# A decoder layer on one core: three transposes moved from TensorE to VectorE and DMAs, the last FFN block in 512 columns, norm2's factor in ScalarE's copies

## The chip, the cores and the metric

The kernel runs on one core of one Trainium2 chip. The core has five engines that run their own instruction streams and meet at semaphores: TensorE (matmuls; PE in the profile, and PEld for its weight loads), VectorE (DVE), ScalarE (ACT), GpSimd (POOL) and SyncE (SP), whose queue issues nearly all DMAs here. The metric is the device time of one execution in microseconds. Lower is better.

## The reference

One layer on `x` of 256 tokens by 1024 channels, in float32:

- `h = rmsnorm(x)`, and `u = h @ W_in`, whose columns are the recurrent input and gate, q, k, v and two branch gates.
- Branch A: a causal depthwise convolution of width 4, a gated linear recurrence over positions, times the GELU of its gate.
- Branch B: attention with 8 heads of 128 channels. With 256 tokens and blocks of 256, it is plain causal softmax attention on normalised q and k.
- `merged = sigmoid(gA) * (A @ P_A) + sigmoid(gB) * (B @ P_B)` and `x = x + merged @ W_out`.
- `h = rmsnorm(x)`, `up = conv3(h @ W_up)` (causal, depthwise, width 3), `act = gelu(up) * (h @ W_gate)`, `x = x + act @ W_down`, with 2816 hidden channels.

## The kernel before, in words

**Matmuls in three parts.** Every float32 operand is split in a high part `hi` (rounded to the matmul type fp32r) and a rest `lo`; a product is three matmuls, high by high, high by low and low by high (`mm3`). Weights stream from HBM in chunks of 128 x 2048 (1 MB): `raw` is loaded, ScalarE copies it to `hi` and VectorE subtracts to get `lo` (`split_part`). There are three `raw`, four `hi` and three `lo` buffers. Activations are split the same way (`split2`).

**Token-major work and turning.** Most projections hold 128 tokens' activations as the stationary operand and pass 512 columns of weights (`tm_mm`; one chunk is 24 matmuls). Their result has tokens in the partitions, while the next product needs channels there, so it is turned. There are two ways. TensorE transposes 128 x 128 blocks against the identity, into a PSUM bank, from which it is split: this is done for the probabilities (`att_t`, three blocks a head, tile `pt`), for the gated sum (`m_t`, four groups of four blocks, tile `mT`) and for norm2's input (`norm2_t`, four groups of four, tile `h2T`). Or `turn` (L437) does it: VectorE transposes 32 x 32 blocks inside the partitions, four DMAs write the strips to DRAM with the partition groups exchanged, and one DMA reads all back. This is done for the recurrent input and gate, q, k, and for the FFN's up and gate products.

**Attention.** For each head, `att_s` makes scores and softmax, `att_t` (L790) the turned and split probabilities, and `att_o` (L800) the output, six matmuls into tile `o`. A head has 384 columns of probabilities, because the causal mask leaves out one block of four.

**norm2's factor.** The rows of `h` aren't scaled before the FFN. Their factor `rs2` is applied afterwards. For up, which has a convolution and a GELU, it is needed along the free axis of the turned product, so `norm2_bcast` (L993) builds a diagonal and multiplies by ones on TensorE (tile `rbfp`), and `pair_up` (L1022) multiplies the turned product by it. For the gate it is left until `add_out` (L1062), where the down product is scaled and added to `x`.

**FFN.** The 11 blocks of 256 hidden channels run in five pairs, each two chunks of up and two of gate in 512 columns (`pair_half`, L1071), and down projections two pairs later (`downs`, L1084). The eleventh block runs alone in `last_block` (L1093), near the end, with the weights as the stationary operand and 256 tokens as columns: 96 matmuls of 256 columns, tiles `upl` and `gtl`, whose results need no turning.

**The order.** All operations are recorded first and then issued by a list written out in the file, `ORDER` (L161): plain numbers are operations of the other engines, `+n` stands for the next n matmuls. TensorE's own order comes from `UNITS` (L34), and `AFTER` (L36) names the items that are recorded after a quarter of a unit (`"pr1.0": "O5"`). Each engine runs its part of the list strictly in order, SP too, so a DMA that waits holds those behind it.

Of the kernel before, what the change touches and what calls it, by code (L numbers as in the profile page):

```python
# [14 lines left out]
P = 128  # L15
S = 256
# [16 lines left out]
KEPT = {"upd": 2, "gtd": 2, "u": 1, "c": 2, "ah": 3, "al": 3}  # L33
UNITS = ("rx0 rx1 rx2 rx3 rg0 rg1 rg2 rg3 k0 k1 k2 k3 ri0 q0 q1 ri1 ga0 ga1 q2 q3 v0 v1 ga2 ga3 v2 v3 gb0 "  # L34
         "gb1 gb2 gb3 pr0 pr1 pr2 pr3 pa0 pa1 pa2 pa3")
# [37 lines left out]
    "ga2.2": "s22 S0 P3",  # L73
# [3 lines left out]
    "ga3.2": "lc1 P1 lb0",  # L77
    "ga3.3": "s26",
    "v2.1": "P0 qrs1 S4",
    "v2.2": "O3 s27 s28",  # L80
    "v2.3": "ld1",
    "v3.2": "S5",
    "gb0.0": "P2",
    "gb0.1": "s29",
    "gb1.0": "gelu0 P4",
    "gb1.3": "s30 S6",
    "gb2.1": "S7",
    "gb2.2": "O2 lc0",
    "gb2.3": "O1 s31 s32 ld0",
    "gb3.0": "ya0",  # L90
    "gb3.1": "P5 ys0",
    "gb3.2": "O4",
    "pr0.0": "P7 sb0 s33",
    "pr0.2": "sa1 ya1",
    "pr0.3": "ys1",
    "pr1.0": "O5",
    "pr1.1": "s34",
    "pr1.2": "sa0",
    "pr1.3": "s35",
    "pr2.0": "P6",  # L100
    "pr2.1": "s36",
    "pr2.2": "O6",
    "pr2.3": "O0",
    "pr3.0": "s37",
    "pr3.3": "sb1",
    "pa1.0": "O7",
    "pa2.1": "m0",
    "pa3.2": "s38",
    "wo.0": "s39 m1",
    "wo.4": "m2",  # L110
    "wo.5": "s40",
    "wo.6": "m3",
    "wo.12": "n00",
    "wo.13": "n10",
    "wo.14": "s41",
    "up00.0": "s42 n01",
    "up00.2": "n11",
    "gt00.0": "s43",
    "gt00.3": "s44",
    "up01.3": "s45 s46",  # L120
    "gt01.2": "s47",
    "gt01.3": "bcast2",
    "up10.0": "ur0 s48",
    "up10.1": "s49",
    "up11.0": "s50",
    "up11.2": "fu0",
    "gt10.0": "s51",
    "gt10.1": "s52 gr0",
# [24 lines left out]
    "dn5.2": "gr4",  # L153
    "dn5.3": "s71",
    "dn7.0": "fg4",
    "last.2": "s72",
# [5 lines left out]
0-2 +1 3-4 +1 5 +1 6 +1 8 +1 7 +1 9 +1 11 +2 10 25 +1 12 30 +1 26-27 +1 14 +1 28 33 +1 29 +1 13 31 +2 32 +2 34 +1  # L162
35 +3 15 +7 36 +2 41 +3 19 +3 37 63 +1 42 +1 39 +3 43 +1 40 +1 17 38 +3 44 +1 49 +2 18 +3 45 64 50 +1 47 +4 51 46
+2 16 48 +3 52 +1 57 +4 53 +1 58 +1 55 +4 59 54 +2 56 +3 60 +7 66 +4 68 +1 67 +5 69 +3 99 +3 65 +5 70 100 +5 71 +5
72 +1 98 73 +1 74 +1 75 +1 76 +1 77 +1 78 104 +1 79-80 +1 81 +1 82 +1 83 +4 84 +1 105 +2 85 +4 116 +4 86 +1 103 +3
# [6 lines left out]
+6 188 228 +1 235 +4 189 +1 308 +2 242 190 +3 191 +2 162 240 +1 192 243 +2 244 247 +1 248 193 239 +1 249-250 +1  # L172
245 251 +2 246 +1 252 271 +2 272 +1 253 +1 229 +2 254 232 +1 309 +2 233 255 +2 230 +1 256 +2 322 +1 257 +2 231 +1
258 307 +2 234 +1 259 +3 260 273 +1 274-275 +1 276 108 261 +3 262 297 +2 323 +1 109 +1 263 329 +2 110 +3 277 +1
111 +3 112 +1 278 +6 299 279 +1 301 +1 321 +3 280 +2 332 330 +2 281 +3 282 +3 283 312 +2 311 302 +1 284 328 314 +2
264 313 305 285 +2 316 303 265 +1 286 315 +1 304 +1 317 +1 266 306 287 +1 318 +1 118 +1 288 +2 333 267 347 +1 289
+1 268 +2 194 269 +3 195 +2 298 196 +3 197 +1 300 +1 270 +1 198 +1 354 331 +1 355-356 +1 357 291 358 +3 290 359
# [8 lines left out]
+3 472 +1 391 +1 428 392 +1 393 +1 476 +3 478 +7 466 +1 473-474 467 +1 439 +2 468 +3 469 +1 527 470 +2 471 +5 484  # L186
+3 485 +2 479 +1 492 +3 494 +2 499 +6 486 528 +1 477 +3 496 +2 429 497 +2 537 +2 487 +1 539 +4 500 +3 507 +9 540
+1 502 498 +1 488 +1 503 +2 210 +1 489 +1 490-491 +2 431 +6 493 432 +4 495 +4 509 +2 510 +3 532 508 +12 504 538 +1
# [8 lines left out]
639 +3 655 +1 657 +9 668 653 +1 669-670 +1 671 +1 672 +1 673 +1 674 +1 675 +1 676 +1 658 +1 660 +9 677 +1 656 678  # L197
# [102 lines left out]
def trunk_layer(ctx: ExitStack, tc: tile.TileContext, xT, x, vec, win_fm, win_tm, wri, wpr, wpa,  # L300
# [58 lines left out]
    c_wo = [add(wout[c]) for c in range(4)]  # L359

    NP = NF // 2
    c_up, c_gt, c_dn = {}, {}, []
    for p in range(NP):
        for c, kh in ((c_up, 0), (c_gt, 0), (c_up, 1), (c_gt, 1)) if p == 0 else (
                (c_up, 0), (c_up, 1), (c_gt, 0), (c_gt, 1)):
# [835 lines left out]
```

## Time and profile before

| | us |
|---|---|
| median of 3 runs (435.06 to 435.16) | 435.13 |
| the profiled execution | 435.01 |
| its span in the trace | 433.2 |
| TensorE busy | 428.4 |
| VectorE busy | 326.8 |
| ScalarE busy | 256.9 |
| GpSimd busy | 50.1 |

The rows below name a line, an engine, an operation and tiles (`out<-in`). Nearly every operation is issued from one line of a helper, L296, so tiles tell the operations apart. Matmuls overlap in TensorE's pipeline: the duration of one is longer than the distance to the next. In the chain of waits a row has the start, the time until the next piece of the chain, the engine, the tile and the number of instructions merged.

### The profile page before, as it was taken

How to read it: one execution, taken by the hardware profiler on the slowest of the kernel's cores; microseconds unless marked ns; L12 is line 12 of the kernel's file. 1: busy time of each engine (PE TensorE's matmuls, PEld its weight loads, DVE VectorE, ACT ScalarE, POOL GpSimd, SP SyncE). 2: the span in 40 equal slices, each digit the busy share in tenths (PEclk: the TensorE clock that was granted, in tenths of full speed). 3: DMA queues.
4: the chain of work that ended last, by engine and by line, in shares of the span. 5: the costliest groups of instructions: out<-in, count | busy, mean ns of one | idle time of the engine just before them, and what ended most of it. 6: DMA issues, size and time to landing. Idle time of an engine off the chain costs nothing.

```text
span 433.2 us, 5466 instructions
## 1 busy us (share of the span) xinstructions
PE 428.4 (99%) x2044; PEld 360.0 (83%) x2044; DVE 326.8 (75%) x426; ACT 256.9 (59%) x285; POOL 50.1 (12%) x101
## 2 busy tenths in 40 slices
PE   8999999999999999999999999999999999999996
PEld 8888888888888888888888888888888888888985
DVE  3877499799888898985666896496979766767643
ACT  4687596886779999963431453357455555355410
POOL 0021007767660000000000000000000000000000
PEclk9999999999999999999999999999999999999999
DMA  7998944889991752274454466888789787697202
GB/s 259 404 385 243 360 153 147 269 292 326 372 358 52 276 194 97 98 290 130 163 194 141 151 220 202 288 288 300 238 264 328 256 285 245 211 317 249 97 2 97
DMA packets 32826, 100.06 MB, mean 231 GB/s; under 512 B 3104, under 2 KB 13472, under 8 KB 29088
## 3 DMA queue, kind: packets, MB, share of 16 engines
q1 hardware_dynamic: 32656, 99.71, 67.1%
q8 instruction: 16, 0.26, 0.2%
q14 instruction: 10, 0.08, 0.1%
q10 hardware_dynamic: 144, 0.00, 0.0%
HBM read 89.22 MB, written 10.49 MB: 230 GB/s over the span
## 4 chain that ended last, share of the span: by engine, by line
PE 97%; DMA 1%; DVE 0%; SPq 0%; ACT 0%; issue 0%
PE acc L296 14%; PE up L296 13%; PE gt L296 13%; PE pr L296 5%; PE gb L296 5%; PE yo L296 5%; PE ga L296 5%; PE v L296 5%; PE pa L296 5%; PE q L296 5%; PE k L296 5%; PE rg L296 5%; PE rx L296 4%; DMA raws<-in_win_fm 1%; PE gtl L296 1%; PE upl L296 1%
## 5 line engine op out<-in xcount | busy, mean ns | idle before, releaser
L296 DVE TENSOR_TENSOR lo<-raw,hi 128x2048 fp32r<-128x2048 f32 (+1 forms) x72 | 160.0, 2224 | 27.2 <-issue 9.5
L296 ACT CAST hi<-raw 128x2048 fp32r<-128x2048 f32 (+1 forms) x69 | 128.4, 1863 | 87.0 <-PE up L296 11.5
L296 PE MATMUL up<-hi,h2h 128*128 128x512 f32 x80 | 31.4, 393 | 0.0
L296 PE MATMUL up<-hi,h2l 128*128 128x512 f32 x80 | 31.1, 389 | 0.0
L296 PE MATMUL acc<-hi,fah 128*128 128x512 f32 x80 | 31.1, 389 | 0.0
L296 PE MATMUL acc<-lo,fah 128*128 128x512 f32 x80 | 31.1, 389 | 0.0
L296 PE MATMUL gt<-hi,h2l 128*128 128x512 f32 x80 | 31.1, 389 | 0.0
L296 PE MATMUL gt<-hi,h2h 128*128 128x512 f32 x80 | 31.1, 389 | 0.0
L296 PE MATMUL gt<-lo,h2h 128*128 128x512 f32 x80 | 31.1, 389 | 0.0
L296 PE MATMUL acc<-hi,fal 128*128 128x512 f32 x80 | 31.1, 389 | 0.0
L296 PE MATMUL up<-lo,h2h 128*128 128x512 f32 x80 | 31.1, 389 | 0.0
L296 ACT ACT_TABLE_LOAD x14 | 18.0, 1283 | 3.1 <-PEq L1191 1.2
L296 DVE SCALAR_TENSOR_TENSOR fc<-fu,pv,fc 128x255 f32<-128x255 f32 (+1 forms) x40 | 17.0, 475 | 2.0 <-ACT fc L296 1.9
L296 POOL TENSOR_TENSOR rsq<-rsq 128x8 f32<-128x8 f32 x32 | 17.1, 533 | 11.8 <-DVE rsq L296 9.6
L296 PEld LDWEIGHTS acc<-hi,fal 128*128 128x128 f32 x80 | 15.0, 188 | 3.2
L296 PEld LDWEIGHTS gt<-hi,h2h 128*128 128x128 f32 x80 | 15.0, 188 | 3.1
L296 PEld LDWEIGHTS up<-hi,h2l 128*128 128x128 f32 x80 | 15.0, 188 | 3.1
L296 PEld LDWEIGHTS acc<-hi,fah 128*128 128x128 f32 x80 | 15.0, 188 | 3.1
L296 PEld LDWEIGHTS gt<-lo,h2h 128*128 128x128 f32 x80 | 15.0, 188 | 3.1
L296 PEld LDWEIGHTS gt<-hi,h2l 128*128 128x128 f32 x80 | 15.0, 188 | 3.1
L296 PEld LDWEIGHTS up<-hi,h2h 128*128 128x128 f32 x80 | 15.0, 188 | 3.0
L296 PEld LDWEIGHTS acc<-lo,fah 128*128 128x128 f32 x80 | 15.0, 188 | 3.0
(228 smaller groups left out, 1041.3 us busy)
## 6 DMA issues: line engine op xcount, KB each, us to landing
raw<-in_win_fm SPq DMA_DIRECT2D x12, 1024.0 KB, 7.6
raw<-in_win_tm SPq DMA_DIRECT2D x12, 1024.0 KB, 6.2
raw<-in_wup SPq DMA_DIRECT2D x11, 1024.0 KB, 5.5
raw<-in_wgate SPq DMA_DIRECT2D x11, 1024.0 KB, 7.7
raw<-in_wdown SPq DMA_DIRECT2D x11, 1024.0 KB, 7.0
raw<-in_wpr SPq DMA_DIRECT2D x4, 1024.0 KB, 4.9
raw<-in_wpa SPq DMA_DIRECT2D x4, 1024.0 KB, 4.9
raw<-in_wout SPq DMA_DIRECT2D x4, 1024.0 KB, 4.8
```

The source lines that it names most:

```text
L296: getattr(engine, name)(*map(real, a), **{n: real(v) for n, v in k.items()})
```

## The change

The probabilities, half of the gated sum and half of norm2's input are no longer transposed by TensorE.

- `att_t` transposes 32 x 32 blocks on VectorE (384 columns) and writes four strips to DRAM; a new item `R` reads them back and a new item `Q` splits them. `att_o` reads the split probabilities, and writes its bank, in pieces of 32 or 64 columns, because the turned data stand in another order.
- The first half of the gated sum (`mt`, `mr`, `ms`) goes through `turn`. For that, the attention projections `pa0` and `pa1`, which complete the first half, run before `pr3`, and `m_t` remains for the second half.
- `W_out` is projected as a unit like the others (`wo0` to `wo3`), one half of its columns after the other, with its chunks loaded by columns in two DMAs. The first column half of `x` is still transposed by TensorE (`norm2_t`); the second goes through a turn (`ht`, `hr`) and is scaled by norm2's gain in four ScalarE copies (`hs`). The FFN's first units are put in an order that uses the second half last.
- `scaled` takes any factor; `ffn_half` uses it to copy up and gate products from PSUM times `rs2` on ScalarE before the turn, which then takes one transpose of 1024 columns in place of two of 512. `norm2_bcast`, with its two products on TensorE, is gone, `pair_up` copies in place of multiplying, and `add_out` adds without a factor.
- The last block's up and gate are one unit of 512 columns (256 of each) that follows the fifth pair and goes through a turn of its own (`lr5`, `fu`, `fg`).
- `UNITS`, `AFTER` and `ORDER` are new throughout.

```diff
-         "gb1 gb2 gb3 pr0 pr1 pr2 pr3 pa0 pa1 pa2 pa3")
+         "gb1 gb2 gb3 pr0 pr1 pr2 pa0 pa1 pr3 pa2 pa3 wo0 wo1 wo2 wo3")
...
+    def by_columns(w, c):
+        cs = slice(c // 2 * 512, c // 2 * 512 + 512)
+        return [w[2 * (c % 2) + j].rearrange("p (k c) -> p k c", k=2)[:, :, cs] for j in range(2)]
...
+            return [(n[:2], int(n[2]), int(n[3])) for n in "up00 gt00 up10 up01 gt01 up11 gt10 gt11".split()]
...
-    def scaled(name, ps):
-        r = half(name)
+    def scaled(r, ps, rs):
         for t in range(2):
-            nc.scalar.activation(r[:, t * 512:(t + 1) * 512], ps[t], AF.Copy, scale=rs1[:, t:t + 1])
+            nc.scalar.activation(r[:, t * 512:(t + 1) * 512], ps[t], AF.Copy, scale=rs[:, t:t + 1])
...
     def att_t(h):
         sm = heads[h]
-        ps = bank(f"pt{h}")
-        for b in range(3):
-            nc.tensor.transpose(ps[:, b * P:(b + 1) * P], sm[:, b * P:(b + 1) * P], ident)
+        d = small(f"pd{h}", 384)
+        nc.vector.transpose(d.rearrange("p (j u b) -> p u j b", j=4, u=3), sm.rearrange("p (u j b) -> p u j b", u=3, j=4))
+        mid = dram.tile([P, 384], F32, tag="pt", name=f"pm{h}")
+        m = mid.rearrange("(j a) (i f) -> i a j f", j=4, i=4)
+        for i in range(4):
+            nc.sync.dma_start(m[i], d[32 * i:32 * i + 32, :].rearrange("p (j f) -> p j f", j=4))
+        heads[h] = d, mid
+    def att_r(h):
+        nc.sync.dma_start(*heads[h])
+    def att_p(h):
         pth, ptl = small(f"pth{h}", 384, F32R), small(f"ptl{h}", 384, F32R)
-        split2(pth, ptl, ps[:, :3 * P])
+        split2(pth, ptl, heads[h][0])
...
+    def m_turn():
+        turn("mm", turned_m, sgb.half(0), "mr")
+    def m_split():
+        v = lambda a: a.half(0).rearrange("p (u i b) -> p u i b", u=8, i=4)
+        split2(v(mh), v(ml), by_tile(turned_m))
...
+    def h2_turn():
+        turn("hm", turned_h, [xs[:, t, halves[1]] for t in range(2)], "hr")
+    def h2_split():
+        m = half("h2p")
+        for k in range(4):
...
+            nc.scalar.activation(kt(m)[:, k, :].rearrange("p (t i b) -> p t i b", t=2, i=4), d, AF.Copy,
+                                 scale=pv[:, V_G2 + 4 + k:V_G2 + 5 + k])
+        split2(h2h.half(1), h2l.half(1), m)
...
-    def norm2_bcast():
+    def norm2_stats():
         nc.vector.tensor_add(ss2[:, 0, :], ss2[:, 0, :], ss2[:, 1, :])
         rsqrt(ss2[:, 0, :], rs2, 1.0 / D, 2)
-        for t in range(2):
-            nc.vector.tensor_scalar(dg[:, t, :], ident, rs2[:, t:t + 1], None, op0=OP.mult)
...
-            nc.tensor.matmul(ps[:, t * P:(t + 1) * P], ones, dg[:, t, :], start=True, stop=True)
-        nc.scalar.copy(rbf, ps[:, :S])
...
-            nc.vector.tensor_mul(plain(u, t), d[:, t], rb[:, t, None].to_broadcast([P, 4, 4, 32]))
+            nc.vector.tensor_copy(plain(u, t), d[:, t])
...
-        nc.vector.scalar_tensor_tensor(xs[:, t, cs], ps, rs2[:, t:t + 1], xs[:, t, cs], op0=OP.mult, op1=OP.add)
+        nc.vector.tensor_add(xs[:, t, cs], ps, xs[:, t, cs])
...
-                turn(f"{kind}m{p}", d, open_ps[kind, p], f"{kind[0]}r{p}")
+                turn(f"{kind}m{p}", d, scaled(keep("s", p), open_ps[kind, p], rs2), f"{kind[0]}r{p}")
...
-    def last_block():
-        pu, pg = fm_ps("upl"), fm_ps("gtl")
-        for ps, i in ((pu, c_up[NP]), (pg, c_gt[NP])):
...
+        if p == NP - 1:
+            for kh in range(2):
+                run(f"last{kh}", ffn_half("last", NP, kh, c_last[kh]))
```

More of the change, by code (lines that the diff above doesn't have):

```diff
@@ L72 @@
     "ga2.1": "rq1 S1 Tq1",
[L73 removed]
+    "ga2.2": "s22 S0",
     "ga2.3": "s23",
@@ L76 @@
     "ga3.1": "lb1",
-    "ga3.2": "lc1 P1 lb0",
+    "ga3.2": "lc1 lb0",
     "ga3.3": "s26",
[L79 to L83, printed above, removed]
+    "v2.1": "qrs1 S4",
+    "v2.2": "s27 s28 P3",
+    "v2.3": "ld1 R3",
+    "v3.2": "S5 R0 P1",
+    "gb0.0": "Q1 P2",
     "gb0.1": "s29",
-    "gb1.0": "gelu0 P4",
+    "gb1.0": "gelu0 R4",
     "gb1.3": "s30 S6",
     "gb2.1": "S7",
[L88 to L93, printed above, removed]
+    "gb2.2": "lc0 R5 P6",
+    "gb2.3": "s31 s32 ld0",
+    "gb3.0": "ya0 O2 Q5 R6",
+    "gb3.1": "ys0 Q6 P7",
+    "gb3.2": "R7",
+    "pr0.0": "sb0 s33",
     "pr0.2": "sa1 ya1",
-    "pr0.3": "ys1",
-    "pr1.0": "O5",
-    "pr1.1": "s34",
+    "pr0.3": "ys1 O5",
+    "pr1.1": "s34 O6",
     "pr1.2": "sa0",
     "pr1.3": "s35",
[L100 to L107, printed above, removed]
-    "pa3.2": "s38",
[L109 to L128, printed above, removed]
+    "pr2.1": "s36 O7",
+    "pa1.0": "s37",
+    "pa1.3": "mt sb1",
+    "pr3.2": "mr",
+    "pa2.3": "ms",
+    "pa3.2": "s38",
+    "v3.0": "Q3",
+    "v3.1": "P0",
+    "v3.3": "Q0 R1",
+    "gb0.2": "R2 O3",
+    "gb0.3": "Q2 P4",
+    "gb1.1": "O0",
+    "gb1.2": "Q4",
+    "gb2.0": "O1 P5",
+    "gb3.3": "O4 Q7",
+    "wo0.0": "s39",
+    "wo0.1": "m2",
+    "wo0.2": "m3",
+    "wo1.0": "s40",
+    "wo2.0": "n00 s41",
+    "wo2.1": "n10",
+    "up00.0": "s42 ht",
+    "up00.3": "s43 hr",
+    "gt00.2": "hs",
+    "up10.0": "s44 s45",
+    "up01.0": "s46 stats2",
+    "gt01.0": "s47",
+    "up11.0": "s48 ur0",
+    "gt10.0": "s49 s50",
+    "gt10.2": "s51 fu0",
+    "gt11.0": "s52 gr0",
     "gt11.1": "ur1",
@@ L152 @@
     "dn4.1": "s70 fg3",
-    "dn5.2": "gr4",
+    "dn5.2": "lr5 gr4",
     "dn5.3": "s71",
-    "dn7.0": "fg4",
-    "last.2": "s72",
+    "dn7.0": "fu fg fg4",
     "dn8.0": "s73",
@@ L381, in load_next @@
         raw[i] = wp.tile([P, 2048], F32, tag="raw", name=f"raw{i}")
+        if isinstance(stream[i], list):
+            n = 2048 // len(stream[i])
+            for a, src in enumerate(stream[i]):
+                d = raw[i][:, a * n:(a + 1) * n]
+                nc.sync.dma_start(d.rearrange("p (k c) -> p k c", k=2) if len(src.shape) == 3 else d, src)
+            return
         if len(stream[i].shape) == 3:
@@ L405, in advance @@
             j = split_tiles()
-            n, m = min(2048, stream[j].shape[-1] * (2 if len(stream[j].shape) == 3 else 1)), {4: 2}.get(j, 1)
+            src = stream[j]
+            n = 2048 if isinstance(src, list) else min(2048, src.shape[-1] * (2 if len(src.shape) == 3 else 1))
+            m = {4: 2}.get(j, 1)
             for a in range(m):
@@ L624, in rx_evac @@
         turned_x[g] = half(f"xd{g}")
-        turn(f"xm{g}", turned_x[g], scaled(f"xs{g}", rx_ps[g]), f"rx{g}")
+        turn(f"xm{g}", turned_x[g], scaled(half(f"xs{g}"), rx_ps[g], rs1), f"rx{g}")
     def rx_order(g):
@@ L816, in rg_evac @@
     def rg_evac(g):
-        turn(f"gm{g}", gr.half(g), scaled(f"gs{g}", rg_ps[g]), f"rgr{g}")
+        turn(f"gm{g}", gr.half(g), scaled(half(f"gs{g}"), rg_ps[g], rs1), f"rgr{g}")
     def gelu(h):
@@ L897, in run_unit @@
             for k4 in range(4):
-                tm_mm(ps, i, 4 * kh + k4, k4, *{"pr": (yah, yal), "pa": (ybh, ybl)}.get(kind, (xgh, xgl)),
-                      kind not in "qkv")
+                tm_mm(ps, i, 4 * kh + k4, k4, *{"pr": (yah, yal), "pa": (ybh, ybl), "wo": (mh, ml)}.get(kind, (xgh, xgl)),
+                      kind not in ("q", "k", "v", "wo"), *((m_stat,) if kind == "wo" else ()))
                 if kh and k4 == 3:
@@ L915, in trunk_layer @@
     for h in range(H):
-        for n, fn in (("S", att_s), ("P", att_t), ("O", att_o)):
+        for n, fn in (("S", att_s), ("P", att_t), ("R", att_r), ("Q", att_p), ("O", att_o)):
             item[f"{n}{h}"] = lambda fn=fn, h=h: fn(h)
-    for n in range(4):
+    for n in (2, 3):
         item[f"m{n}"] = lambda n=n: m_t(n)
+    item["mt"], item["ms"] = m_turn, m_split
     def run(name, quarters):
@@ L943, in trunk_layer, with norm2, squares @@
     rs2 = const.tile([P, 2], F32, name="rs2")
-    def norm2(t, hf):
-        cs = halves[hf]
-        nc.vector.tensor_add(xs[:, t, cs], yo[t, hf], xs[:, t, cs])
+    def norm2(hf, ps):
+        for t in range(2):
+            nc.vector.tensor_add(xs[:, t, halves[hf]], ps[t], xs[:, t, halves[hf]])
+    def squares(t, hf):
+        nc.scalar.activation(small(f"sq2{t}{hf}", 512), xs[:, t, halves[hf]], AF.Square,
+                             accum_out=ss2[:, hf, t:t + 1])
+    turned_h = half("hd")
+    def h2_turn():
[3 more added lines that the diff above has]
+        for k in range(4):
+            d = turned_h.rearrange("p (i t c b) -> p c t i b", i=4, t=2, c=4)[:, k]
+            nc.scalar.activation(kt(m)[:, k, :].rearrange("p (t i b) -> p t i b", t=2, i=4), d, AF.Copy,
+                                 scale=pv[:, V_G2 + 4 + k:V_G2 + 5 + k])
+        split2(h2h.half(1), h2l.half(1), m)
+        for t in range(2):
+            squares(t, 1)
     def norm2_t(t, hf):
@@ L958, in norm2_t @@
         split2(kt(h2h.half(hf))[:, :, ts], kt(h2l.half(hf))[:, :, ts], m)
[L959 to L980 removed]
+        squares(t, hf)
     for t in range(2):
[L983 to L984 removed]
+        item[f"n{t}0"] = lambda t=t: norm2_t(t, 0)
+    item["ht"], item["hs"] = h2_turn, h2_split
     for kind, c in units:
@@ L987, in trunk_layer @@
             run(f"{kind}{c}", run_unit(kind, c))
-    run("wo", out_proj())
-    rbf = const.tile([P, S], F32, name="rbf")
-    rbf2 = rbf[:, None, :].to_broadcast([P, 2, S])
-    def norm2_bcast():
+    def norm2_stats():
         nc.vector.tensor_add(ss2[:, 0, :], ss2[:, 0, :], ss2[:, 1, :])
         rsqrt(ss2[:, 0, :], rs2, 1.0 / D, 2)
-        for t in range(2):
-            nc.vector.tensor_scalar(dg[:, t, :], ident, rs2[:, t:t + 1], None, op0=OP.mult)
-        ps = psA.tile([P, 512], F32, tag="A", name="rbfp")
-        for t in range(2):
-            nc.tensor.matmul(ps[:, t * P:(t + 1) * P], ones, dg[:, t, :], start=True, stop=True)
-        nc.scalar.copy(rbf, ps[:, :S])
     acc, act, kept = {}, {}, {}
@@ L1040, in pair_gate, with last_up, last_gate @@
             act[2 * p + i] = tuple(kt(a[:, i * 512:(i + 1) * 512]) for a in (ah, al))
-    def up_post(j, ps):
-        uc = half(f"fuc{j}")
-        u, c = kt(uc[:, :512]), kt(uc[:, 512:])
-        nc.vector.tensor_mul(u, ps, rbf2)
-        for i in range(2):
-            conv3(c[:, i, :], u[:, i, :], 2 * j + i)
-        nc.scalar.activation(c, c, AF.Gelu_apprx_tanh)
-        return c
-    def gate_post(j, c, ps):
-        nc.vector.tensor_mul(c, c, ps)
-        a = half(f"fa{j}", F32R)
-        act[j] = (kt(a[:, :512]), kt(a[:, 512:]))
-        split2(*act[j], c)
+    lu = half("flu")
+    lc = lu[:, 512:]
+    def last_up():
+        for t in range(2):
+            nc.vector.tensor_copy(plain(lu[:, :512], t), turned["last"][:, t, :2])
+        for i in range(2):
+            conv3(kt(lc)[:, i, :], kt(lu[:, :512])[:, i, :], 2 * (NF - 1) + i)
+        nc.scalar.activation(lc, lc, AF.Gelu_apprx_tanh)
+    def last_gate():
+        for t in range(2):
+            nc.vector.tensor_mul(plain(lc, t), turned["last"][:, t, 2:], plain(lc, t))
+        a = half("fla", F32R)
+        act[NF - 1] = (kt(a[:, :512]), kt(a[:, 512:]))
+        split2(a[:, :512], a[:, 512:], lc)
+    item["fu"], item["fg"] = last_up, last_gate
     def down(j, t, hf):
@@ L1067, in trunk_layer, with ffn_half @@
         item[f"fg{p}"] = lambda p=p: pair_gate(p)
-    item["n11"] = lambda: norm2_t(1, 1)
-    item["bcast2"] = norm2_bcast
-    def pair_half(kind, p, kh):
-        c = (c_up if kind == "up" else c_gt)[p, kh]
+    item["stats2"] = norm2_stats
+    def ffn_half(kind, p, kh, c):
         if not kh:
-            open_ps[kind, p] = [bank(f"{kind}{p}{t}") for t in range(2)]
+            open_ps[kind, p] = [psA.tile([P, 512], F32, tag="A", name=f"{kind}{p}{t}") if p == 1 else bank(f"{kind}{p}{t}")
+                                 for t in range(2)]
         advance(c)
@@ L1078, in pair_half @@
             if kh and k4 == 3:
-                d = keep(kind + "d", p)
-                turn(f"{kind}m{p}", d, open_ps[kind, p], f"{kind[0]}r{p}")
-                turned[kind, p] = d.rearrange("p (i t c b) -> p t c i b", i=4, t=2, c=4)
+                d = half("fld") if kind == "last" else keep(kind + "d", p)
+                turn(f"{kind}m{p}", d, scaled(keep("s", p), open_ps[kind, p], rs2), f"{kind[0]}r{p}")
+                turned["last" if kind == "last" else (kind, p)] = d.rearrange("p (i t c b) -> p t c i b", i=4, t=2, c=4)
             yield
@@ L1091, in downs @@
                 yield
[L1093 to L1111 removed]
+    for p in range(NP):
+        for kind, n, kh in ffn_order(p):
+            run(f"{kind}{n}{kh}", ffn_half(kind, n, kh, (c_up if kind == "up" else c_gt)[n, kh]))
+        if p == NP - 1:
+            for kh in range(2):
+                run(f"last{kh}", ffn_half("last", NP, kh, c_last[kh]))
         if p >= 2:
@@ L1116, in trunk_layer @@
     run(f"dn{2 * NP - 3}", downs(2 * NP - 3))
-    run("last", last_block())
     run(f"dn{NF - 3}", downs(NF - 3))
```

107 lines of the change are left out of this document (37 added, 70 removed), and 82 rows, old and new, of the table ORDER.

## The prediction

> **What bounds the kernel now.** I read the page's busy times first, then who TensorE waits for, then the chain that ended last, and last the two stages in which another engine is nearly full.
>
> ```profile
> span 433.2 us, 5466 instructions
> PE 428.4 (99%) x2044; PEld 360.0 (83%) x2044; DVE 326.8 (75%) x426; ACT 256.9 (59%) x285; POOL 50.1 (12%) x101
> PE warm L296 <- DVE ones L296: 1.0, 1, 1.0
> PE rx L296 <- ACT his L296: 0.2, 1, 0.2
> PE 97%; DMA 1%; DVE 0%; SPq 0%; ACT 0%; issue 0%
> ```
>
> TensorE is busy 428.4 of 433.2 us and its only waits are 1.2 us at the start. The chain is TensorE from 10.67 us to the last result. So a TensorE instruction that goes is worth its place in that chain, as long as nothing new makes TensorE wait. Busy time can't price it, because matmuls overlap (a 512-column one lasts 389 ns and starts every 227); the chain's rows can, because each begins where the one before it ends:
>
> ```profile
> 128.15 0.69 PE s L296 x6
> 128.84 0.33 PE pt L296 x3
> 129.17 5.51 PE ga L296 x24
> ...
> 183.45 0.64 PE o L296 x6
> ...
> 189.65 0.33 PE pt L296 x3
> ...
> 215.34 0.44 PE mT L296 x4
> 215.78 8.21 PE pa L296 x36
> ...
> 234.49 0.43 PE mT L296 x4
> ...
> 243.11 0.44 PE h2T L296 x4
> ...
> 252.65 0.44 PE h2T L296 x4
> ...
> 254.46 5.44 PE gt L296 x24
> ...
> 270.79 0.44 PE rbfp L296 x4
> 271.24 10.91 PE up L296 x48
> ...
> 401.82 5.75 PE upl L296 x48
> 407.58 5.76 PE gtl L296 x48
> 413.34 14.99 PE acc L296 x66
> ...
> 429.79 0.48 DVE xs L296
> ```
>
> **What leaves TensorE.** (a) The probabilities: `pt` stands eight times, 0.33 us each: 2.64. (b) The gated sum: two of four `mT` groups, 0.88. (c) norm2's input: two of four `h2T` groups, 0.88. (d) norm2's factor: `rbfp`, 0.45 (270.79 to 271.24). (e) The last block: 96 matmuls of 256 columns took 5.75 + 5.76 = 11.51; 48 of 512 columns take twice the 5.44 that 24 take at 254.46, 10.88: 0.63 less. (f) A run that follows such a group starts late: 5.51 for 24 after `pt` against 5.44, 10.91 against the 10.88 just named after `rbfp`. At 0.02 to 0.07 for each of the 13 groups that go, I take 0.45. Sum 5.93. At the end the add no longer scales: 0.48 us against 0.42 for an equally large plain sum (row below), 0.06. Together **6.0 us** off the chain.
>
> **What it adds to TensorE.** The eight `o` groups keep their six matmuls, but read the probabilities and write their bank in pieces of 32 or 64 columns. No row has the written pieces. The nearest rows with moving data in pieces of 32 are the score groups, 0.69 us at 128.15, against 0.64 for `o` at 183.45: so 0 to 0.05 each, 0 to 0.4 in all; the same columns pass, so nothing in it can be quicker. I take 0.2, the middle. The projection `wo` changes the order of its loops and keeps its 96 matmuls: 0.
>
> **What it adds beside TensorE, and where that may show.**
>
> ```profile
> 130.00:190.00 60.00, 60.00 (x301) 50.38 (x300) 53.73 (x91) 58.83 (x81) 0.00 (x0) 1.00 0.45 163
> 260.00:430.00 170.00, 169.75 (x802) 142.64 (x800) 120.12 (x136) 77.82 (x64) 0.00 (x0) 1.00 0.69 231
> L296 DVE STREAM_TRANSPOSE fgtd<-gt 128x512 f32<-128x512 f32 x10 | 7.1, 709 | 7.2 <-DMA upm<-fupd 5.3 <-PE gt L296 1.9
> L296 DVE STREAM_TRANSPOSE xd<-xs 128x1024 f32<-128x1024 f32 x2 | 2.5, 1238 | 0.5 <-ACT xs L296 0.5
> L296 DVE TENSOR_TENSOR ybl<-o,ybh 128x256 fp32r<-128x256 f32 x8 | 3.3, 418 | 1.2 <-ACT ybh L296 1.0
> L296 ACT ACTIVATE gs<-rg,rs 128x512 f32<-128x512 f32 x4 | 2.7, 682 | 4.5 <-PE rg L296 4.5
> 178.66 1.05 ACT L296 CAST yah<-it 128x1024 fp32r<-128x1024 f32 x1
> 179.74 1.23 DVE L296 TENSOR_TENSOR yal<-it,yah 128x1024 fp32r<-128x1024 f32 x1 [0.62 <-ACT yah L296]
> 182.38 0.39 PE L296 MATMUL pr<-hi,yal 128*128 128x512 f32 x1
> 158.87 1.28 ACT L296 ACT_TABLE_LOAD   x1
> 160.16 1.06 ACT L296 ACTIVATE gr<-gr 128x1024 f32<-128x1024 f32 x1
> ```
>
> FFN, 260 to 430 us (first columns of a window's row: TensorE, weight loads, VectorE, ScalarE): eleven turns get two scaled copies, 22 of 0.68 = 15 us on ScalarE, which is busy 78 of 170. VectorE loses two transposes of 0.71 a turn for one of 1.24. That work is hidden by the distance between a turn and its down projection: the last gate product is split at 402.8 us in the row below and first used by `acc` at 413.34. A turn becomes 1.4 us longer; without that cover it would cost 1.4 each time. I take 0.
>
> ```profile
> 401.54 1.22 DVE L296 TENSOR_TENSOR fal<-fc,fah 128x1024 fp32r<-128x1024 f32 x1
> ```
>
> Attention, 130 to 190: here ScalarE is busy 58.83 of 60 and VectorE 53.73. Each head's 384-column transpose (between the two rows above, 0.58) adds 4.6 us to VectorE; the splits stay. The emitted order holds 15 table loads where there were 14, and the additional one lies among those of attention and gates: 1.28 on ScalarE. TensorE, rid of seven `pt` groups before `yal` is needed, gets there 2.6 us sooner (seven times 0.33, and 0.25 of the late starts of (f)), and `yal` was done at 180.97, 1.4 before its use at 182.38. What is short: 2.6 + 1.28 - 1.4 = 2.5, less what ScalarE has idle in the stage, 1.17: **1.3 us**. In the new order head 5's split (for `o`) and `yal` stand behind one another on VectorE, so I expect the wait at one of them. Bounds: 0, if the new order uses VectorE's 6.3 us of idle time better; 4, if the transposes lie in ScalarE's chain too and a third of them shows. The load at 158.87 ends at 160.15 and the next activation starts at 160.16, so nothing follows a load. The Trainium skill ("ScalarE: Activation LUTs", "What ACT_TABLE_LOAD costs") counts a drain of some 1.38 us behind each load; by that the wait would be an estimated 2.7 and the time 431.9, and the row speaks against it.
>
> The queue: 61 more DMAs on SP, 40 of them for heads, 15 for three new turns (gated sum, norm2's input, last block), 6 because `wo` and the last block load a chunk in two. SP waited in order before, so a read that waits for its four writes holds the weight loads behind it:
>
> ```profile
> SPq L296 <- DVE lo L296: 238.7, 61, 12.8
> 86.17 1.78 SPq L296 DMA_DIRECT2D gm<-gr  x4
> raw<-in_wout SPq DMA_DIRECT2D x4, 1024.0 KB, 4.8
> upm<-fupd SPq DMA_DIRECT2D x20, 128.0 KB, 6.0
> fupd<-upm SPq DMA_DIRECT2D x5, 512.0 KB, 5.3
> DMA to landing us min/median/max: 2.3/5.1/9.4
> ```
>
> It spends 238.7 us waiting for a buffer to come free, so 61 issues of some 0.45 (1.78 for four) fit: 0. The tightest new path is norm2's second half. From the end of `wo` to its first use TensorE has three units of 5.44 = 16.3 us. The path: two sums and two transposes of 512 columns, 0.7 each, 2.8; four issues 1.8; write and read to landing; four scaled copies (at most 0.68) 2.7; a split, like `yah` and `yal`, 2.3: 9.6 and the two landings. So write and read may take 6.7 us together. The quickest landing of the `gm` turn is 2.3 (last row); the FFN medians 6.0 + 5.3 = 11.3 were behind megabyte loads, while `wout` loads landed in 4.8, nearly free of others. I take 2.5 + 4 = 6.5: no wait, but without room. The gated sum has 16.3 us too, and 8.1 of other work (four products and sums 2.8, a transpose 1.2, issues 1.8, a split 2.3): 8.2 for its landings.
>
> Sum against the profiled run, 435.01 us (span 433.2; the median of the runs is 435.13): 435.01 - 6.0 + 0.2 + 1.3 = **430.5**.
>
> **Rivals.** (1) *All hidden.* The attention order has room; TensorE waits nowhere: 429.0 to 429.5. For it: TensorE hasn't waited once in a stage with ScalarE 98% busy. Against: 1.2 us of idle time on ScalarE. (2) *ScalarE becomes the bound* from 130 to 190: the 1.17 us aren't to be had, and the earlier TensorE comes, the more it waits; 2.5 to 4 us: 431.7 to 433.2. (3) *Slower: landings.* One mechanism: turned data share the DMA engines with megabyte loads, and TensorE waits at `up01` and `wo`. What write and read take beyond 6.7 and 8.2 us is added; at 11.3 that is 4.6 + 3.1 = 7.7, and 438.2. It decides from 9.7 us, where the two excesses, 3.0 + 1.5, use up the 4.5 gained. For it: the FFN medians. Against: `wout` loads, the ones in flight there, land in 4.8. The Trainium skill, "DMA: Bandwidth & Descriptors", "Specifications", says that under 512 B a transfer is read, modified and written; the probabilities' pieces are 384 B. No trace here shows such a turn; a head's turn has some 15 us between its transpose and `o`, so even a doubled landing changes neither sum nor chance. (4) *The change does not do what it says*: the time of the turns comes back as waits for `o` in full, 435.
>
> **How the numbers follow.** The forecast (a wait of 0.7 to 2.2 in attention, 429.7 to 431.3) has 0.48; (1) 0.22; (2) 0.20; (3) 0.06; (4) 0.04. The range runs from 428.5 (no wait, nothing on `o`, late starts at 0.07 in place of 0.035) to 433.4 (a wait of 4, `o` at 0.4) and leaves (3) and (4) out, 0.10. A measurement of this kernel can tell 0.2%, 0.87 us. Faster: the forecast, (1), (2), and a third of (3): 0.92. Same, within it: most of (4) and the edge of (3), 0.04. Slower: the rest, 0.04.
>
> **What would show it.** `pt` and `rbfp` gone from the chain, `mT` and `h2T` at two groups; `last` about 10.9 us; TensorE's waits: 1 to 2 us near 180 us, at `o` or `pr`, released by VectorE, and none behind 190. Wrong would make it: a wait at `wo` or `up` released by a DMA or the split behind one (3), waits spread over all heads (2), or an `o` group well over 0.70 us.

## The result, and the profile after

| | before | changed |
|---|---|---|
| median of 6 runs, us | 435.14 (434.94 to 435.60) | 430.06 (428.91 to 433.33) |
| ratio to before | | 0.9897, 95% interval 0.9880 to 0.9914 |
| the profiled execution, us | 435.01 | 433.33 |
| its span in the trace, us | 433.2 | 431.5 |

The change saves 5.1 us between the medians, 1.2%; by the ratio it is 1.0%. Its runs lie 4.4 us apart, those of before 0.7, and the profiled execution is the slowest of the six. A second profile of the same kernel (last but one of the experiments) took 429.94 us.

The page of the changed kernel, the waits of TensorE, and rows of its chain of waits:

```profile
span 431.5 us, 5421 instructions
PE 424.5 (98%) x1952; PEld 354.3 (82%) x1952; DVE 328.8 (76%) x424; ACT 271.6 (63%) x309; POOL 50.9 (12%) x101
PE 71%; DMA 11%; ACT 10%; DVE 3%; issue 2%; SPq 2%; ACTq 0%; DVEq 0%
PE o L300 <- DVE ptl L300: 2.4, 1, 2.4
PE pr L300 <- DVE yal L300: 0.2, 1, 0.2
```

```profile
155.78 7.78 DMA raw<-in_wpr
163.58 1.17 ACT hi L300
...
184.16 4.02 PE pr L300 x10
188.18 0.65 PE o L300 x6
...
379.21 10.88 PE last L300 x48
...
428.27 0.43 DVE xs L300
```

`pt` and `rbfp` are gone from the chain, and the last block takes 10.88 us where it took 11.51. What is new is a stretch of the chain that isn't TensorE's: it leads through a wait of 2.4 us at head 5's `o` and 0.2 at `yal` to ScalarE, and from there to a load, the first chunk of `W_proj`. Behind 190 us TensorE waits for nothing. In order of time, from the timelines of SP, ScalarE and TensorE (start, duration, engine, then the idle time in front and what ended it):

```profile
148.55 0.34 SPq L300 DMA_DIRECT2D pd<-pm  x1
149.00 1.82 SPq L300 DMA_DIRECT2D pm<-pd  x4
153.95 0.34 SPq L300 DMA_DIRECT2D pd<-pm  x1
154.34 1.40 SPq L300 DMA_DIRECT2D pm<-pd  x3
155.78 0.43 SPq L300 DMA_DIRECT2D raw<-in_wpr  x1
```

```profile
163.58 1.91 ACT L300 CAST hi<-raw 128x2048 fp32r<-128x2048 f32 x1 [2.90 <-DMA raw<-in_wpr]
```

```profile
180.03 0.28 PE L300 MATMUL o<-pth,vh 128*128 128x256 f32 x1
182.69 0.39 PE L300 MATMUL o<-ptl,vh 128*128 128x256 f32 x1 [2.38 <-DVE ptl L300]
184.16 0.79 PE L300 MATMUL pr<-hi,yal 128*128 128x512 f32 x1 [0.16 <-DVE yal L300]
186.46 0.63 PE L300 MATMUL pr<-lo,yah 128*128 128x512 f32 x1
```

SP issues in order. The reads of turned probabilities (`pd<-pm`) wait at 148.55 and 153.95 us until their strips have landed, and the load of `W_proj`'s first chunk stands behind them until 155.78. ScalarE then stands 2.90 us for it, VectorE's split of head 5 follows ScalarE's, and TensorE waits. After the wait its 512-column matmuls last 0.63 us in place of 0.39: the granted clock has fallen. The window's last figures are clock, DMA share and GB/s:

```profile
184.00:186.00 2.00, 1.84 (x5) 1.49 (x5) 2.00 (x3) 1.98 (x4) 0.00 (x0) 0.50 0.94 254
180.00:190.00 10.00, 7.46 (x31) 5.69 (x30) 10.00 (x10) 9.97 (x15) 0.00 (x0) 0.83 0.62 202
```

### The profile page after: what moved, and what is told of

It reads as the page before. It is cut to its first block, busy times and chain, and to the rows that moved or that the text cites. A ratio compares the mean times of both kernels' runs of the same rounds, so it can differ in the third digit from the quotient of the medians.

```text
span 431.5 us, 5421 instructions
## 1 busy us (share of the span) xinstructions
PE 424.5 (98%) x1952; PEld 354.3 (82%) x1952; DVE 328.8 (76%) x424; ACT 271.6 (63%) x309; POOL 50.9 (12%) x101
## 4 chain that ended last, share of the span: by engine, by line
PE 71%; DMA 11%; ACT 10%; DVE 3%; issue 2%; SPq 2%; ACTq 0%; DVEq 0%
PE acc L300 14%; PE gt L300 13%; PE up L300 13%; PE wo L300 5%; PE rg L300 5%; PE pa L300 5%; PE k L300 5%; PE rx L300 4%; PE pr L300 4%; ACT hi L300 3%; DMA raw<-in_win_tm 3%; DMA pm<-pd 3%; PE last L300 3%; ACT L300 2%; DMA raw<-in_wpr 2%
## 5 line engine op out<-in xcount | busy, mean ns | idle before, releaser
L300 ACT ACTIVATE fc<-fu,pv 128x256 f32<-128x256 f32 x20 | 10.8, 593 | 15.9 <-DVE fu L300 15.9
L300 POOL TENSOR_TENSOR rsq<-rsq 128x8 f32<-128x8 f32 x32 | 15.9, 498 | 31.4 <-DVE rsq L300 29.3
L300 PEld LDWEIGHTS up<-lo,h2h 128*128 128x128 f32 x80 | 15.0, 188 | 3.1
```

Source lines behind the costliest of these rows:

```text
L300: getattr(engine, name)(*map(real, a), **{n: real(v) for n, v in k.items()})
```

## The experiments

Theory at the start: TensorE gets its 6 us, and what is lost of them is one wait in attention, made by SP's order. Rivals: (B) ScalarE's own work, (C) VectorE's eight added transposes. Where an edit adds or takes away operations, the numbers in `ORDER` shift; the cuts below leave that out.

**The load moved ahead.** In `ORDER`, 466 is the load, 497 the read of head 0's probabilities.

```diff
-... 463 +1 465 +1 516 +2 464 +1 466 525 ...
+... 463 +1 465 +1 516 +2 464 +1 525 ...
-... 578 +3 497 ...
+... 578 +3 466 497 ...
```

> One issue changes place on SP's queue: the load of W_proj's first chunk (raw, in_wpr) goes ahead of the read of head 0's turned probabilities, which in the changed kernel held it until 155.78 us. Theory (the queue: SP holds the load, ScalarE then stands 2.90 us for want of it at 163.58, and VectorE's split of head 5, which follows ScalarE's, comes 2.4 us late for TensorE): ScalarE's idle time before that copy goes, the waits at head 5's o and at yal go (2.4 and 0.2 us become at most 0.5 together), the clock stays at 0.99 or more there, and the time is 427.5 to 429, in all runs alike. Rival B (ScalarE has simply too much to do, the additional table load above all): ScalarE idles less but the wait stays above 1.5 us, 429.5 to 431. Rival C (VectorE's eight added transposes are what is late): the wait stays as it is, 2.4 us, 430.

Measured: 431.6 us (431.33 to 433.64), ratio 0.9942 (0.9926 to 0.9958): slower than the change as it was. TensorE still waits 2.1 us at `o`. The load now left at 146.55 us. SP's and ScalarE's timelines say what it did:

```profile
146.55 0.39 SPq L299 DMA_DIRECT2D raw<-in_wpr  x1
149.28 0.34 SPq L299 DMA_DIRECT2D pd<-pm  x1
149.67 2.10 SPq L299 DMA_DIRECT2D pm<-pd  x4
157.15 0.34 SPq L299 DMA_DIRECT2D pd<-pm  x1
```

```profile
154.81 0.51 ACT L299 CAST pth<-pd 128x384 fp32r<-128x384 f32 x1 [1.90 <-DMA pd<-pm]
```

The probabilities are late instead: a read that went at 153.95 now goes at 157.15, behind a megabyte, and ScalarE stands 1.90 us for one of them. So order alone isn't the cause: in these two orders, whichever of load and strips goes second lands late and keeps ScalarE standing.

**Less work on ScalarE.** 530 and 210 are the two GELUs of the recurrent gate. 530 ran first, near 137 us; the edit puts it behind, beside 210, near 147. The load is where it was.

```diff
-... 378 142 +1 530 377 ...
+... 378 142 +1 377 ...
-... 402 +1 401 +1 210 ...
+... 402 +1 401 +1 530 210 ...
```

> The GELU of the second half of the gate moves up beside the first half's, so ScalarE loads its tables 13 times in place of 15, 2.57 us less of its work before head 5; the load of W_proj stays behind the read. Rival B (ScalarE's work sets the wait): the wait at head 5's o shrinks by those 2.5 us, to 0.3 us or less, and the time is 427.5 to 429. Theory (the queue): the copy of W_proj's first chunk still has to wait for its data until 163.58 us, ScalarE only idles longer in front of it, and the wait at o stays 2 us or more: 429.5 to 431. Rival C: the wait stays, 430.

Measured: 430.3 us (429.49 to 432.6), ratio 0.9908 (0.9890 to 0.9926): nothing gained. ScalarE is busy 269.0 us against 271.6, the price of two table loads, and stands 0.76 us at the same copy, which starts at 161.69; the wait at `o` is 0.6. So rival B's numbers didn't come, and neither did the theory's copy at 163.58 and wait of 2 us. Nor did the work taken away turn into idle time in front of the load: in the second profile of the changed kernel ScalarE stands 0.72 us there, and from 148.65 us up to that copy the rows of both start within 0.3 us of each other. The time went earlier, into two waits for VectorE's maxima that the second profile doesn't have:

```profile
137.67 0.49 ACT L299 ACTIVATE sm<-sm,mx,rq 128x128 f32<-128x128 f32 x1 [1.62 <-DVE mx L299]
142.44 0.49 ACT L299 ACTIVATE sm<-sm,mx,rq 128x128 f32<-128x128 f32 x1 [0.65 <-DVE mx L299]
```

VectorE held ScalarE back as soon as ScalarE had less to do. By the drain that the Trainium skill ("ScalarE: Activation LUTs", "What ACT_TABLE_LOAD costs") counts with each load, two fewer should have given an estimated 5.3 us; the 2.6 agree with the 1.28 of the trace, and around the load at 145.44 us no drain shows: the copy before it ended at 145.42, and the activation behind it starts at 146.74, 0.02 after its end.

**What a transpose costs TensorE, and where.** 24 transposes are added, six at the start of each of four units, first in the FFN, then in attention ahead of `o`. In the second kernel the identity matrix is built earlier, on GpSimd.

```diff
+        if not kh and kind in ("up", "gt") and p in (2, 3):
+            for b in range(6):
+                nc.tensor.transpose(open_ps[kind, p][b // 3][:, b % 3 * P:(b % 3 + 1) * P], ident, ident)
...
+            if (kind, c) in (("ga", 2), ("v", 2), ("gb", 0), ("gb", 2)):
+                for b in range(6):
+                    nc.tensor.transpose(ps[b // 3][:, b % 3 * P:(b % 3 + 1) * P], ident, ident)
```

> The changed kernel with 24 transposes of 128 columns more on TensorE, six at the start of up and gate of the third and fourth FFN pairs, into banks that the next matmul overwrites: as many as the probabilities had before. There TensorE never waits. If a transpose group costs its place in the chain (0.33 for three, and some hundredths of a late start behind each), the time rises by 2.6 to 2.9 us over the changed kernel, to about 432.9. If the transposes hide in TensorE's pipeline between longer matmuls, it rises by less than 1.5 us.

> The same 24 transposes, but in the attention stage, six at the start of four units between 129 and 170 us, ahead of head 5's o. If TensorE there only waits for ScalarE and VectorE, whose work doesn't begin earlier or later for that, the 2.6 us that the transposes take are taken from the wait: the waits at head 5's o and yal fall from 2.6 to under 0.7 us, the clock stays up, and the time is that of the changed kernel within 0.7 us, 429.5 to 430.7. If the wait moves along with TensorE (because what ScalarE waits for is set free by TensorE), the time rises by 2.6 us, to 432.7, and the wait stays.

Measured in the FFN: 433.33 us (432.37 to 435.35), ratio 0.9978 (0.9965 to 0.9990), 3.3 us over the changed kernel's median. Two rows of its chain, one of 48 matmuls and one of 48 and six transposes:

```profile
278.38 10.89 PE gt L299 x48
289.27 11.57 PE up L299 x54
```

0.68 for six; the four groups, 11.57, 11.56, 11.57 and 11.56 less 10.88 each, make 2.74. A transpose group costs its place in the chain. Between the two profiled executions (433.13 us, and 429.94 in the second profile of the changed kernel) the rest lies at the start: the one chain reaches TensorE at 10.92 us, the other at 10.36.

Measured in attention: 431.58 us (431.25 to 431.66), ratio 0.9929 (0.9916 to 0.9942), 1.5 over the changed kernel, and the runs are 0.4 us apart. The wait list names nothing in attention, and ScalarE copies `W_proj`'s chunk without standing. The split of head 5 and its first use, and the copy:

```profile
179.76 0.55 DVE L299 TENSOR_TENSOR ptl<-pd,pth 128x384 fp32r<-128x384 f32 x1
```

```profile
183.00 0.28 PE L299 MATMUL o<-ptl,vh 128*128 128x256 f32 x1
```

```profile
161.19 1.90 ACT L299 CAST hi<-raw 128x2048 fp32r<-128x2048 f32 x1
```

Two things follow. The time without any wait, with the price of the transposes taken from the run before, is an estimated 431.58 - 2.74 = 428.8 us, 5.8 below the 434.65 that before took on that chip. And without the transposes TensorE would be at `o` at 183.00 - 2.74 = 180.26, where the split ends at 180.31: with its data in time, the work of ScalarE and VectorE fits TensorE's to 0.1 us. My expectation of no more than 0.7 over was wrong, because it took the recorded wait of 2.6 for the usual one; most runs have less to give.

**The probabilities' DMAs taken away.**

```diff
-            nc.sync.dma_start(m[i], d[32 * i:32 * i + 32, :].rearrange("p (j f) -> p j f", j=4))
+            pass
...
-        nc.sync.dma_start(*heads[h])
+        pass
```

> Left out: the forty DMAs of the turned probabilities. Each head's split reads the transposed tile before its strips have been exchanged, so the attention part of the output is another one; the work of TensorE, VectorE and ScalarE is the same, instruction by instruction. Revised theory (ScalarE's and VectorE's work in attention fits to within some 0.2 us, and the wait at head 5's o is what the landing of W_proj's first chunk or of the probabilities makes ScalarE stand): the wait falls to 0.3 us or less, the clock stays up, and the time is 428.7 to 429.4, with the runs within 0.8 us of each other where the changed kernel's were 4.4 apart. Rival B (the work itself is too much): the wait stays at 1 us or more and the time at 430.

Measured: 429.43 us (428.98 to 429.91), ratio 0.9872 (0.9859 to 0.9885). TensorE's waits in attention:

```profile
PE pr L297 <- DVE yal L297: 0.2, 1, 0.2
PE o L297 <- DVE ptl L297: 0.2, 1, 0.2
```

As the theory has it, at the edge of its numbers: same work, no late data, 0.4 us of waiting, clock 1.00, runs 0.9 us apart. By the ratios (the change has 0.9897 above and 0.9904 in a second measurement below) the DMAs' lateness costs 0.25 to 0.32%, 1.1 to 1.4 us; by the medians, each against its own before, 0.5 to 1.2 us. The intervals touch, so its size isn't settled.

**The probabilities' DMAs on GpSimd's queue**, alone and with the GELU moved.

```diff
-            nc.sync.dma_start(m[i], d[32 * i:32 * i + 32, :].rearrange("p (j f) -> p j f", j=4))
+            nc.gpsimd.dma_start(m[i], d[32 * i:32 * i + 32, :].rearrange("p (j f) -> p j f", j=4))
...
-        nc.sync.dma_start(*heads[h])
+        nc.gpsimd.dma_start(*heads[h])
```

> The forty DMAs of the turned probabilities are issued by GpSimd, which has nothing to do from 130 to 190 us; SP keeps the weights, and issues W_proj's first chunk when its buffer is free, near 146.5 us. Theory: SP's order was what kept either the chunk or the probabilities late; in a queue of their own the strips pass beside the megabyte load, no wait of more than 0.5 us is left, 428.7 to 429.6. Rival (the sixteen DMA engines are what both share, so strips wait behind a load wherever they are issued): as with the load moved ahead, where the probabilities landed late and ScalarE stood 1.9 us for them: 431 to 432.

> The two edits together: the probabilities' DMAs on GpSimd's queue, and the second GELU beside the first, with two table loads (2.57 us) less on ScalarE. Theory: with the data in time ScalarE gains the 2.57 us as slack, TensorE waits nowhere in attention, and all runs lie at 428.5 to 429.2. Rival (DMA engines shared): the slack takes up most of the late landing, 429 to 430.5.

Measured: 436.91 us (435.59 to 438.24), ratio 1.0042 (1.0025 to 1.0059), and with the GELU 1.0051 (1.0030 to 1.0072): both slower than before the change, and beyond the ranges of theory and rival. Rows of GpSimd's timeline, of the chain, and of the list of queues:

```profile
152.47 2.18 POOL L299 DMA_DIRECT2D pm<-pd  x4
159.39 0.57 POOL L299 DMA_DIRECT2D pd<-pm  x1 [4.74 <-DMA pm<-pd]
```

```profile
146.20 5.16 DMA pm<-pd
...
154.10 4.71 DMA pm<-pd
```

```profile
q0 software_dynamic: 1536, 3.15, 2.4%
```

Four issues take 2.18 us there and 1.82 on SP, and the last strips of two heads need 5.16 and 4.71 us from their issue to their landing, against 4.47 and 3.51 at the same places of the changed kernel (143.96 and 150.39 us in its chain). The Trainium skill ("DMA: Bandwidth & Descriptors", "Queues, rings and completion order") has the DMA engines take turns between queues, packet by packet; that spoke for the theory, and here a queue of its own did not make the strips quicker. GpSimd issues in order too, so a read that waits 4.74 us for its strips holds the next head's strips there as on SP, and it still built the identity matrix in between (0.85 us at 144.37 and 145.62). Its DMAs also run in a queue of another kind, `q0 software_dynamic`, where SP's is `q1 hardware_dynamic`. How much of the loss is contention with the loads and how much GpSimd's queue itself, no run separates.

**Twice the transposes on VectorE.**

```diff
+        for _ in range(2):
+            nc.vector.transpose(d.rearrange("p (j u b) -> p u j b", j=4, u=3), sm.rearrange("p (u j b) -> p u j b", u=3, j=4))
-        nc.vector.transpose(d.rearrange("p (j u b) -> p u j b", j=4, u=3), sm.rearrange("p (u j b) -> p u j b", u=3, j=4))
```

> Each of the eight transposes of probabilities on VectorE is made twice, 8 x 0.58 = 4.6 us more of its time, in the stage where it is busy 9.3 to 9.8 of 10 us. Rival C (VectorE is what makes TensorE wait): the wait at head 5's o grows by 2 to 4.6 us, and the time is 432 to 435. Theory (ScalarE and what it waits for set the wait; VectorE has room where ScalarE stands): less than 1 us more, 430 to 431.

Measured: 434.62 us (433.5 to 436.83), ratio 1.0000 (0.9985 to 1.0016). TensorE's wait and a row of ScalarE's timeline:

```profile
PE o L299 <- DVE ptl L299: 2.9, 1, 2.9
```

```profile
158.22 0.50 ACT L299 ACTIVATE sm<-sm,mx,rq 128x128 f32<-128x128 f32 x1 [1.82 <-DVE mx L299]
```

4.6 us of VectorE's time came with 4.6 us more: I had expected less than 1, and rival C's numbers came. That the two figures are equal is chance: against the second profile of the changed kernel the wait at `o` is 2.2 us longer, the stretch from there to the next head's `o` 1.2 (5.03 against 3.88, with the granted clock at 0.83 from 180 to 190 us), 0.5 lies at the start, and the rest in small pieces. ScalarE waits for VectorE's maxima, so the two make one chain through attention. VectorE has no room either; with the eight transposes of the change the chain just fits, with eight more it doesn't.

**Half the load ahead.** The chunk is loaded in two DMAs; the first goes where the whole was ahead, the second stays behind the read.

```diff
+        if i == 30:
+            for c in range(2):
+                nc.sync.dma_start(raw[i][:, c * 1024:(c + 1) * 1024], stream[i][:, c])
+            return
```

> W_proj's first chunk is loaded as two DMAs of 512 KB: the first goes ahead of the read of head 0's probabilities, where the whole chunk was in the run with the load moved ahead, the second stays where the chunk was, behind that read. Theory (the wait at head 5's o is what ScalarE stands for data: for the chunk when the chunk is behind, for the probabilities when the whole chunk is ahead of their strips): half a chunk delays the strips by half as long, and the other half lands some 2.5 us sooner than the chunk did, so ScalarE stands less than 0.6 us for either, the wait is at most 0.4 us, the clock stays up, and the time is 428.8 to 429.6, close to the run without the forty DMAs. Rival (any byte ahead of the strips costs what it saves behind them): 430 to 431.5.

> The same, and the second GELU beside the first (two table loads, 2.57 us, less on ScalarE). Alone this edit gave nothing, because ScalarE then stood longer for W_proj's chunk. Theory: with the chunk there in time the 2.57 us become room, and all runs lie at 428.5 to 429.2. If ScalarE's work doesn't matter even then, because VectorE (which with twice the transposes made TensorE wait 2.9 us) is full as well: as half_ahead without it, within 0.3 us.

> The changed kernel itself, beside the two above on the same chip. Theory: the wait at head 5's o follows ScalarE's idle time ahead of the copy of W_proj's first chunk, in this execution as in the others: idle 0.6 to 0.8 went with a wait of 0.6, idle 2.9 with 2.4. And the clock falls after a wait of 2 us or more (mean 0.83 from 180 to 190 us) and not after one of 0.6. Time 429.5 to 430.5 in the median.

Measured on one chip: the changed kernel 430.25 us (428.45 to 433.40), ratio 0.9904 (0.9878 to 0.9931); half ahead 429.54 (428.97 to 429.72), 0.9879 (0.9864 to 0.9893); half ahead with the GELU 429.59 (429.16 to 430.11), 0.9884 (0.9871 to 0.9896). ScalarE and the wait, in the second profile of the changed kernel:

```profile
161.63 1.92 ACT L300 CAST hi<-raw 128x2048 fp32r<-128x2048 f32 x1 [0.72 <-DMA raw<-in_wpr]
```

```profile
PE o L300 <- DVE ptl L300: 0.7, 1, 0.7
PE pr L300 <- DVE yal L300: 0.2, 1, 0.2
```

and the halved load, with TensorE's only wait in attention:

```profile
146.56 0.36 SPq L299 DMA_DIRECT2D raw<-in_wpr  x1
...
154.55 0.34 SPq L299 DMA_DIRECT2D pd<-pm  x1
...
156.35 0.43 SPq L299 DMA_DIRECT2D raw<-in_wpr  x1
```

```profile
PE pr L299 <- DVE yal L299: 0.2, 1, 0.2
```

Same kernel, two executions: 0.72 us of standing went with a wait of 0.7, and 2.90 with 2.4. In the one the load was issued at 156.04 and its copy began 5.59 us later, in the other, recorded first, 7.80 us after its issue at 155.78. So SP's order decides when the load can go, but how long it then takes differs from execution to execution. Two kernels that are the same up to there fit in: 0.59 and a wait of 0.6 with the transposes in the FFN, and no standing and no wait at `o` in the last experiment below, where the load went at 154.84. With half of it ahead the read of the strips goes at 154.55, ScalarE doesn't stand, and no run comes out near 433 (0.75 us from first to last, against 4.95). In the median this version is 0.7 us quicker than the change, but the intervals of the two ratios overlap. Two of twelve runs of the changed kernel were near 433, and none of the eight with half the load ahead; that is too few to call the smaller spread shown. What the profile shows is that the standing is gone. The GELU adds nothing to it, as it should where VectorE is full too.

**A later landing elsewhere.** norm2's second half is written and read twice.

```diff
-            nc.sync.dma_start(m[i], dst[32 * i:32 * i + 32, :].rearrange("p (j f) -> p j f", j=4))
-        item[read] = lambda: nc.sync.dma_start(dst, mid)
+            for _ in range(1 + (name == "hm")):
+                nc.sync.dma_start(m[i], dst[32 * i:32 * i + 32, :].rearrange("p (j f) -> p j f", j=4))
+        item[read] = lambda: [nc.sync.dma_start(dst, mid) for _ in range(1 + (name == "hm"))]
```

> The turn of norm2's second half is made with each of its four writes twice and its read twice, so that its data come later; nothing else changes. In the changed kernel the split of that half was done 2.4 us before TensorE used it (262.82 and 265.26 us). Four more issues are 1.8 us and a second read 2 to 3.4, so the data come 3.8 to 5.2 us later. If landings there are as the prediction's third rival has them (what they take beyond the room is added to the time), TensorE waits 1.4 to 2.8 us at the first product with the second half, and the time is 431.5 to 433; and if a wait of 2 us or more lowers the clock at any place, 1 to 1.7 us come on top, and the granted clock of the following microseconds falls below 0.9. If the room is larger than it looks (the second read lands with the first): no wait, 430.

Measured: 440.64 us (440.54 to 441.8), ratio 1.0145 (1.0128 to 1.0163). SP's timeline, TensorE's wait and the clock behind it:

```profile
246.91 10.20 SPq L299 DMA_DIRECT2D hm<-hd  x8
```

```profile
PE up L299 <- ACT h2h L299: 7.2, 1, 7.2
```

```profile
265.00:270.00 5.00, 1.51 (x3) 0.80 (x4) 1.23 (x1) 4.36 (x6) 0.00 (x0) 0.50 1.02 362
270.00:275.00 5.00, 5.00 (x13) 3.83 (x13) 2.29 (x1) 2.10 (x2) 0.00 (x0) 0.50 0.95 302
275.00:280.00 5.00, 5.00 (x23) 4.13 (x22) 2.29 (x1) 3.16 (x3) 0.00 (x0) 1.00 0.41 167
```

The delay was larger than meant: a second write to the same strip waited for the first, eight issues took 10.20 us in place of four in 1.8, the second read waited for the first as well (258.96 and 262.14 us in the chain), and the data came at 265.61 where they came at 254.50 in the second profile, 11.1 later. 7.2 of them showed, so the room was some 3.9. Beyond it the third rival's rule holds, and with a surcharge: 22 matmuls behind the wait took 7.79 us (4.99 at 0.227 each), the first two 1.22 (0.45), 3.6 us for the clock.

## Why the prediction was right, and where it wasn't

Forecast 430.5, measured 430.06. The forecast of what leaves TensorE holds; that the wait came out near its 1.3 us is luck, because it was worked out from the wrong cause.

- *What leaves TensorE, 6.0.* Right. The groups are gone from the chain, the last block is at the 10.88 worked out for it, 24 transposes measured 2.74 in place against 2.64 and their late starts, and the kernel without waits comes to 428.8, 5.8 below its own before.
- *`o` in pieces, 0.2.* It costs nothing: 0.64 and 0.65 us a group, as before. The row of the score groups was the wrong neighbour.
- *The wait in attention, 1.3.* The place was right (head 5's split, then `yal`, released by VectorE), and the size in the second profile nearly: 0.7 + 0.2. In the recorded execution it was 2.6, outside the 0.7 to 2.2 of the forecast. The working was not right. It made the wait from ScalarE's work: 2.6 earlier, 1.28 for a table load, less 1.4 and 1.17. Taking 2.57 of that work away changed nothing, because ScalarE then waited 2.3 for VectorE, whose 4.6 of new transposes the sum held only in its upper bound; and with the data in time the work of both fits to 0.1 us. What failed is the next term, **SP's queue at 0**. I had seen that a read holds the weights behind it, and weighed it against 238.7 us of waiting over the whole span, when what counted was one load at 155 us and the 5.6 to 7.8 us it needs. It cost 0.5 to 1.4 us, by the figure that is taken, and in the recorded execution some 2.6 and the clock's 1.5.
- *The clock* stood nowhere in the sum. In the recorded execution ten matmuls behind the wait took 4.02 us; with half the load ahead they took 2.56 (the ten at 181.98).
- *FFN copies on ScalarE, 0.* Right: no wait behind 190 us.
- *Landings.* Right, with more room than I gave them. From the last of norm2's four issues (252.43) the strips were there at 254.22 and the read's data at 257.59: 5.2 us, where I had 6.5 of 6.7. The rows between them, and the split 2.4 us ahead of its use:

```profile
250.62 1.81 SPq L300 DMA_DIRECT2D hm<-hd  x4
254.22 0.34 SPq L300 DMA_DIRECT2D hd<-hm  x1
```

```profile
257.59 1.71 ACT L300 ACTIVATE h2p<-hd,pv 128x256 f32<-128x256 f32 x4 [1.54 <-DMA hd<-hm]
```

- *The rivals.* "All hidden" (429.0 to 429.5) is what the kernel does when the chunk is on time: half ahead and no DMAs took 429.5 and 429.4. "ScalarE becomes the bound" (431.7 to 433.2) has the size of the two late runs of twelve, 433.3 and 433.4, though not the cause of the first; the second has no profile. Landings at `wo` and `up01`, and the full return of the gain, weren't seen.

## What to carry to other kernels

Where a stage has two engines full, don't ask whether another queue has time left over the span, but which of its transfers each full engine needs next, when it can be issued, and what is issued just ahead of it; and remember that moving it ahead makes whatever it passes late. A transfer that fits neither before nor behind may fit in two halves. And count a wait of TensorE of two microseconds or more with what its clock loses afterwards.

## What the hardware showed that I had not expected

The granted clock falls after rather short waits. With 0.7 us (0.6 in two other kernels) it stayed at 1.00 from 180 to 190 us; with 2.1, 2.4 and 2.9 us it was 0.83 there; after 7.2 us it was 0.50 until some 275 us. The fall comes when the wait is over: in the recorded execution the wait ended at 182.69, and the clock was 1.00 from 182 to 183 us, 0.94 from 183 to 184 and 0.50 from 184 to 187. It then cost 1.5 us behind the 2.4, and 3.6 behind the 7.2. The Trainium skill ("TensorE: Matmul & The Clock Gate", "Part 1: The HAM clock gate") has the clock halve after an idle window of some 3.4 us; the 0.50 agrees, but here 2.1 us were enough (and 0.2 soon after, at `yal`).

The strips of the probabilities, in pieces of 384 B, landed in 1.5 us at the quickest (3.8 in the median), norm2's in pieces of 1 KB in 2.1 at the quickest (2.3). The Trainium skill ("DMA: Bandwidth & Descriptors", "Specifications") has a read and rewrite below 512 B. These rows don't tell whether it was paid: the first are 48 KB each, the second 128, and no run changes the pieces alone.
